# A hybrid recurrent layer on one core: the start in a fixed order on four engines, the first scan's set-up and the output groups moved

## The chip, the cores and the metric

The kernel runs on one core of a Trainium2 chip. A core has five engines that work side by side, each through its own queue of instructions in order: TensorE (PE, matrix products; loading the stationary operand is listed apart as PEld), VectorE (DVE), ScalarE (ACT), GpSimd (POOL) and SyncE (SP), which here issues the transfers between DRAM and the on-chip memory. [...] The metric is the device time of one execution in microseconds (us), lower is better.

## The reference

One layer with two mixers runs over a prompt of 1,024 tokens and over 8 samples of 8 tokens each that continue from given states, 1,088 tokens in all, in float32:

```python
xn = rmsnorm(x, g_norm)
proj = xn @ w_in                                  # 1024 -> 7168: xm, zm, om, f, q, i, z
xc, conv_new = causal_conv(xm, conv_buf, conv_w, conv_b); xc = silu(xc)
q, k = xc_h @ w_q, xc_h @ w_k; v = xm_h @ w_v     # 4 heads
gates = concat(q, k, v) @ w_gate + b_gate         # input and forget gate of each head
hm = mlstm_scan(q, k, v, ig, logsigmoid(fg), ...) # chunked; layernorm, om, skip, zm follow
oh = hgrn2_scan(silu(q), k, i, logf, S0)          # 8 heads; rmsnorm, silu(z) follow
y = rmsnorm(x + concat(hm, oh) @ w_out, g_final)  # and the new states
```

`logf` and the second mixer's `k` use lower bounds from a softmax over `lb_param`.

## The kernel before

**Float32 by three products.** A float32 operand is split into a high part of reduced precision (a cast on ACT) and the rest (a subtraction on DVE or POOL); `mm3` (lines 92 to 96) makes high x high, high x low and low x high, accumulated in PSUM. So every operand costs a cast and a subtraction before PE can use it. `wraw`, `whi` and `wlo` are the raw weights and their two parts, in three, two and two buffers; `XH` and `XL` are the two parts of the turned and normed x.

**The start.** Nine tiles of x (128 tokens each, the last 64) come in by SP in an order fixed by `ordered` (line 188): x 0, the constants, `gB` (g_norm spread over 128 partitions by the transfer itself), x 1, x 2, two weight blocks, x 3 to x 8. `x_norm` (line 220) squares on ACT, takes the root on POOL and scales by `gB` on DVE (L229); `x_split` turns the tile on PE (L241), casts it into `XH` on ACT (L245) and puts the rest into `XL` on DVE (L246). Behind them come the parameter rows (`PR`, turned into `PAR`), the lower bounds (`LB`, `OML`, lines 327 to 335), the convolution's and the norm's history (`hist`) and the gate weights (`wgr`, `wgf`).

**The blocks.** `in_block` (line 270) makes 128 of the 7,168 projected columns for all tokens, in three chunks of 384, 384 and 320 tokens (a block is 72 matmuls of eight k steps), and hands each chunk to an `evac`. It loads the block after next and splits the next. The first eight blocks are `xm`, two for each of four heads. `front_conv` (line 453) makes them: ACT copies a chunk into `xmh` and `XB`, DVE makes `xml` (L470); behind the whole block stand the convolution (one L483 and three L486 on DVE), a sigmoid on ACT (L492), the gating on DVE (L494) and the split into `xch`, `xcl` (L498 on POOL). The first call makes two blocks side by side, the others one.

**The heads.** `qkv_prep` (line 384) loads a head's `w_q`, `w_k`, `w_v`, splits them (`wqh`, `wql`) and appends to the value weights the columns that give the gates: turn `w_v` (L402), copy `wT`, multiply by the gate weights (L406), copy `gv` (L409), turn it (L411), cast into `wqh` (L414) and `wql` (L415). `front_v` makes the values of nine token tiles and the gates' first part, `front_qk` queries and keys, and `gate_part` (a burst of small matmuls) the rest of the gates.

**The scans and the output.** Twelve jobs follow (eight `hgrn_main`, four `mlstm_main`); `weave` lets the blocks of the next job run between a job's own small matmuls. `gate_scan` (line 557), which carries the gates of all four mLSTM heads through DRAM and scans them on DVE, runs inside the first job, whose first level needs `Q1`, `K1` and `Sf` (lines 994 to 1014) from DVE. The output product runs in two halves of 512 columns (`hf`), nine token tiles and two groups of k steps each (`out_part`), whose operands `mix_prep` loads and splits (L1302, L1303); `out_done` adds the last k step and the residual, `wo_prep` loads and splits two k steps of `w_out`. The first five tiles of the first half (`EARLY`) run inside the last job.

**Who sets the order.** The program is written down in one sequence, and a planner with a timeline of its own orders each engine's queue from it. `behind`, `inorder`, `burst` and `issue_after` add constraints of order between two instructions of one engine. Under `tc.manual_schedule(engines=...)` the listed engines keep the written order; before the change that holds for PE alone, from the scans on (line 1441).

## Time and profile before

| | us |
|---|---|
| median of 3 runs | 1157.92 |
| range of these runs | 1155.51 to 1158.99 |
| the profiled execution | 1159.27 |
| its span, first to last instruction | 1157.5 |

The page gives PE 1121.6 us busy (97% of the span), DVE 745.1, ACT 467.9, POOL 259.7. In the views below a row of the order of time reads: start, duration, engine, line, operation, written<-read, count, and in brackets the idle time of the engine before it and what ended that. A row of stretches reads: stretch, its length, busy time and instructions of each engine, the granted clock of TensorE as a share, the share of the DMA engines' time, GB/s. A group's row reads: count, busy us in all, mean ns of one, idle time before.

### The profile page before, as it was taken

The page shows a single profiled execution, that of the slowest core. Times are in us where ns is not written, and L with a number is a line of the kernel's source. Part 1 is how long each engine was busy: PE and PEld are TensorE (multiplying, and loading weights), DVE is VectorE, ACT ScalarE, POOL GpSimd, SP SyncE. Part 2 cuts the span into 40 slices and gives each one's busy share as a digit, 9 for nine tenths or more (in the row PEclk, how much of TensorE's full clock was granted, in tenths as well). Part 3 has the DMA queues.
Part 4 walks back from the last instruction along what each step waited for, and adds up shares of the span by engine and source line. Part 5 has one row for each costly group of instructions (what it writes and reads, how often), then busy time and mean ns, then how long its engine had stood idle before and what let it go on. Part 6 is the DMA issues. An engine that isn't in the chain of part 4 may idle for free.

```text
span 1157.5 us, 22938 instructions
## 1 busy us (share of the span) xinstructions
PE 1121.6 (97%) x9251; PEld 1055.4 (91%) x9251; DVE 745.1 (64%) x1474; ACT 467.9 (40%) x1045; POOL 259.7 (22%) x403
## 2 busy tenths in 40 slices
PE   5889999999999999999999999999999999999997
PEld 5789999899999999999999999999999997878886
DVE  4665354394778667784779567877676686644543
ACT  5454454434532444235423453252524354333332
POOL 4352443102530044203530153102020200100000
PEclk9889999999999999999999999999999999999999
DMA  7234343213324152323224331422222255576662
GB/s 250 56 122 143 119 144 126 71 50 117 103 76 146 54 167 73 122 94 127 64 78 151 116 112 60 133 76 77 56 77 56 76 175 144 156 215 177 188 190 93
DMA packets 154296, 134.05 MB, mean 116 GB/s; under 512 B 11515, under 2 KB 130391, under 8 KB 154190
## 3 DMA queue, kind: packets, MB, share of 16 engines
q1 hardware_dynamic: 154190, 132.59, 36.6%
q8 instruction: 73, 1.20, 0.4%
q14 instruction: 33, 0.27, 0.1%
HBM read 93.99 MB, written 38.57 MB: 115 GB/s over the span
## 4 chain that ended last, share of the span: by engine, by line
PE 84%; DVE 6%; DMA 5%; ACT 3%; issue 2%; POOL 0%; SPq 0%; POOLq 0%; DVEq 0%; ACTq 0%
PE mm L94 23%; PE mm L95 23%; PE mm L96 23%; PE lv L101 2%; DMA mraw<-mixd 2%; DMA woraw<-in_w_out 2%; PE o L1190 1%; PE o L1209 1%; PE o L94 1%; PE o L96 1%; PE o L95 1%; PE o L1212 1%; DVE mlo L1303 1%; PE lv L1171 1%; PE o L1104 1%
## 5 line engine op out<-in xcount | busy, mean ns | idle before, releaser
L94 PE MATMUL mm<-XH,whi 128*128 128x384 f32 (+1 forms) x1344 | 450.1, 335 | 2.2 <-DVE xml L470 2.0
L95 PE MATMUL mm<-XL,whi 128*128 128x384 f32 (+1 forms) x1344 | 440.0, 327 | 0.0
L96 PE MATMUL mm<-XH,wlo 128*128 128x384 f32 (+1 forms) x1344 | 439.5, 327 | 0.0
L94 PEld LDWEIGHTS mm<-XH,whi 128*128 128x128 f32 x1344 | 253.8, 189 | 4.8 <-DVE xml L470 2.2
L95 PEld LDWEIGHTS mm<-XL,whi 128*128 128x128 f32 x1344 | 253.7, 189 | 1.6 <-issue 1.3
L96 PEld LDWEIGHTS mm<-XH,wlo 128*128 128x128 f32 x1344 | 253.2, 188 | 0.0
L147 POOL TENSOR_TENSOR wlo<-wraw,whi 128x1024 fp32r<-128x1024 f32 x34 | 83.1, 2445 | 104.7 <-ACT whi L147 104.6
L147 ACT CAST whi<-wraw 128x1024 fp32r<-128x1024 f32 x56 | 58.8, 1050 | 94.5 <-PE mm L95 74.6
L948 POOL MEMSET A<- 128x288 f32 x8 | 2.7, 343 | 261.4 <-ACT A L1077 261.4
L1302 ACT CAST mhi<-mraw 128x1024 fp32r<-128x1024 f32 (+1 forms) x32 | 31.8, 997 | 66.5 <-PE mm L95 42.8
L96 PE MATMUL mm<-XH,mlo 128*128 128x512 f32 x144 | 56.5, 392 | 2.1 <-DVE mlo L1303 2.1
L94 PE MATMUL mm<-XH,mhi 128*128 128x512 f32 x144 | 56.9, 395 | 1.2 <-ACT mhi L1302 1.2
L95 PE MATMUL mm<-XL,mhi 128*128 128x512 f32 x144 | 56.1, 390 | 0.0
L1303 DVE TENSOR_TENSOR mlo<-mraw,mhi 128x1024 fp32r<-128x1024 f32 (+1 forms) x32 | 37.0, 1156 | 20.6 <-ACT mhi L1302 19.4
L470 DVE TENSOR_TENSOR xml<-mm,xmh 128x384 fp32r<-128x384 f32 (+1 forms) x24 | 12.3, 511 | 50.9 <-ACT XB L469 47.9
L896 DVE TENSOR_SCALAR f<-f,OML,LB 128x384 f32<-128x384 f32 (+1 forms) x24 | 32.8, 1368 | 12.0 <-ACT f L894 11.6
L1371 POOL TENSOR_TENSOR rs<-rs,mhalf 128x1 f32<-128x1 f32 (+1 forms) x9 | 4.9, 542 | 148.5 <-DVE rs L1370 148.5
L96 PE MATMUL mm<-woh,mlo 128*128 128x512 f32 x96 | 37.5, 390 | 0.1
L95 PE MATMUL mm<-wol,mhi 128*128 128x512 f32 x96 | 37.4, 389 | 0.0
L94 PE MATMUL mm<-woh,mhi 128*128 128x512 f32 x96 | 37.3, 389 | 0.0
L486 DVE SCALAR_TENSOR_TENSOR Y<-XB,PAR,Y 128x1112 f32<-128x1112 f32 x24 | 36.8, 1533 | 0.3
L964 DVE TENSOR_TENSOR QK<-hk,Sf 128x256 f32<-128x256 f32 x96 | 36.2, 419 | 0.0
(355 smaller groups left out, 2188.3 us busy)
## 6 DMA issues: line engine op xcount, KB each, us to landing
wraw<-in_w_in SPq DMA_DIRECT2D x56, 512.0 KB
woraw<-in_w_out SPq DMA_DIRECT2D x16, 512.0 KB
mraw<-mixd SPq DMA_DIRECT2D x16, 512.0 KB
mraw<-mixd SPq DMA_DIRECT2D x16, 448.0 KB
xcd<-XB SPq DMA_DIRECT2D x8, 544.0 KB
qkd<-qk SPq DMA_DIRECT2D x16, 272.0 KB
xcr<-xcd SPq DMA_DIRECT2D x8, 544.0 KB
mixd<-xcr SPq DMA_DIRECT2D x8, 544.0 KB
```

The costliest lines, as they stand in the source:

```text
L94: PE.matmul(out, lhsT=lh, rhs=rh, start=first, stop=False)
L95: PE.matmul(out, lhsT=lh, rhs=rl, start=False, stop=False)
L96: PE.matmul(out, lhsT=ll, rhs=rh, start=False, stop=last)
L101: i = PE.matmul(out, lhsT=lhsT, rhs=rhs, start=start, stop=stop)
L147: return S.copy(hi, raw), eng.tensor_tensor(lo, raw, f32(hi), op=ALU.subtract)
L470: evs.append(V.tensor_tensor(ml[:, t0:t0 + m], ps[:, :m], f32(mh[:, t0:t0 + m]), op=ALU.subtract))
L486: V.scalar_tensor_tensor(Y[:, :1112], XB[:, j:j + 1112], cw[:, 8 * j + ft:8 * j + ft + 1], Y[:, :1112], op0=ALU.mult, op1=ALU.add)
L896: V.tensor_scalar(f[:, s], f[:, s], scalar1=OML[:, h:h + 1], scalar2=LB[:, h:h + 1], op0=ALU.mult, op1=ALU.add)
L964: i = V.tensor_tensor(dst, ksrc, ssrc, op=ALU.mult)
L1104: PE.transpose(pt[:, u * P:(u + 1) * P], iT[:, t * P:(t + 1) * P], ident)
L1302: S.copy(hi[:, :w * n], raw[:, :w * n])
L1303: V.tensor_tensor(lo[:, :w * n], raw[:, :w * n], f32(hi[:, :w * n]), op=ALU.subtract)
```

## The change

It has these parts.

- **g_norm:** 4 KB go into one partition on ACT's queue (`g1`); two matmuls with a row of ones spread them over 128 partitions, and DVE copies them into `gB`. x 3 is loaded ahead of the second weight block.
- **The start up to the fourth block's end** is written as one sequence and kept on PE, ACT, DVE and POOL. `x_norm` and `x_split` become `x_square`, `x_scale`, `x_turn` and `x_low`; tiles 3 to 8 stand between the k steps of the first two blocks, and so do the parameter rows, the history, the gate weights and each step of `qkv_prep(0)`. The convolutions are generators (`convolve`), whose steps stand among the matmuls that follow.
- **Work between engines:** the low parts of the first three weight blocks and of block 3, head 0's `xcl`, and head 1's `wql` are made on DVE instead of POOL. `qkv_prep(1)`, the second head's, is spread over the third and fourth block; its casts, its turning and its products stand at four places. For the heads behind it, the second step (the splits) follows the load at once, as before.
- **The lower bounds** are made behind the fourth head's gate columns (`ctxs["cast"]`), beside `masks`; the gate biases are loaded behind the fourth block, the parameter rows behind the last x.
- **The scans' set-up:** the first DVE operation of `gate_scan`'s second step stands behind the copy into `Sf` of the first job (`ctxs["k2"]`).
- **The output:** `out_part` makes the operands of the next group ahead of its own matmuls; tiles 5 to 8 of the first half run one after the other with `out_done` of two earlier tiles and two `wo_prep` behind each; `g_final` is loaded ahead of them.

```diff
+    g1 = unit("g1")
+    nc.scalar.dma_start(out=g1[0:1, :DM], in_=g_norm)
-            lambda: nc.sync.dma_start(out=gB[:, :DM], in_=g_norm.to_broadcast([P, DM])), lambda: x_load(1), lambda: x_load(2),
-            lambda: blk_load(0), lambda: blk_load(1), *[lambda t=t: x_load(t) for t in range(3, 9)])
+    last_x = ordered(lambda: x_load(0), lambda: nc.sync.dma_start(out=CF, in_=c_f32), lambda: x_load(1), lambda: x_load(2),
+            lambda: blk_load(0), lambda: x_load(3), lambda: blk_load(1), *[lambda t=t: x_load(t) for t in range(4, 9)])
...
+        behind(V.tensor_tensor(lbm, lbr[:, 0:8], lbr[:, 8:16], op=ALU.max), ctxs["cast"])
...
-        G.tensor_tensor(wl[:, :512], wr[:, :512], f32(wh[:, :512]), op=ALU.subtract)
-        G.tensor_tensor(wlv[:, :, :256], wrv, f32(whv[:, :, :256]), op=ALU.subtract)
+        eng = V if h == 1 else G
+        eng.tensor_tensor(wl[:, :512], wr[:, :512], f32(wh[:, :512]), op=ALU.subtract)
+        eng.tensor_tensor(wlv[:, :, :256], wrv, f32(whv[:, :, :256]), op=ALU.subtract)
...
-            G.tensor_tensor(cl[:, :T], xc[:, :T], f32(ch[:, :T]), op=ALU.subtract)
+        (V if h == 0 else G).tensor_tensor(cl[:, :T], xc[:, :T], f32(ch[:, :T]), op=ALU.subtract)
...
-        V.tensor_tensor(lm[0:4, :], lfs, m0t, op=ALU.add)
+        behind(V.tensor_tensor(lm[0:4, :], lfs, m0t, op=ALU.add), ctxs["k2"])
...
-        mx = ctxs.pop("mix0") if (hf, t, g) == (0, 0, 0) else mix_prep(t, g)
+        mx = mixes.pop((hf, t, g), None) or mix_prep(t, g)
+        if ahead:
+            mixes[ahead] = mix_prep(*ahead[1:])
...
+    with tc.manual_schedule(engines={ET.PE, ET.Activation, ET.DVE, ET.Pool}):
+        ones = g1[0:1, DM:U]
+        G.memset(ones, 1.0)
+        for i in range(2):
+            pt = ps_o()
+            PE.matmul(pt, lhsT=ones, rhs=g1[0:1, i * 512:(i + 1) * 512], start=True, stop=True)
+            V.tensor_copy(gB[:, i * 512:(i + 1) * 512], pt)
+        x_square(0)
+        x_square(1)
+        x_scale(0)
+        x_square(2)
+        x_turn(0)
+        x_scale(1)
+        x_low(0)
+        low = split_high(0)
+        x_turn(1)
+        x_scale(2)
+        x_low(1)
+        low()
+        x_square(3)
+        x_turn(2)
+        x_low(2)
+        x_square(4)
+        low = split_high(1)
+        x_scale(3)
+        low()
+        convs = []
+        first = front_conv(0, (0, 1), convs)
+        run(islice(first, 1))
+        x_turn(3)
+        x_scale(4)
+        x_low(3)
+        x_square(5)
+        run(islice(first, 2))
...
+        x_turn(8)
+        x_low(8)
+        next(prep)
+        par_turn()
+        hist_turn()
+        gate_weights()
+        run(islice(first, 3))
+        next(prep)
+        run(islice(first, 2))
+        next(prep)
+        run(islice(first, 2))
+        blk_split(2, V)
+        run(prep)
+        c0, c1 = convs
+        next(c0)
+        run(islice(first, 4))
+        run(first)
+        next(c0)
+        next(c1)
+        run(front_v(0))
+        next(c0)
+        convs = []
+        third = front_conv(1, (2,), convs)
+        prep = qkv_prep(1)
+        next(prep)
+        run(islice(third, 2))
+        next(c0)
+        next(c1)
+        run(islice(third, 2))
+        next(c1)
+        run(c0)
+        next(c1)
+        run(islice(third, 4))
+        run(c1)
+        next(prep)
+        run(islice(third, 4))
+        run(third)
+        c2, = convs
+        next(prep)
+        front_qk(0)
+        next(c2)
+        next(prep)
...
+        for t in range(EARLY, 9):
+            part_of(0, t)
+            for n in (t - 1, t - EARLY):
+                out_done(0, n)
+                for i in islice(wos, 1):
+                    wo_prep(1, i)
```

## The prediction

> **What bounds the kernel now.** I read four views in this order: the page (shares, slices, chain), the waits of TensorE alone, the busy time of stretches that I cut at the clock's changes, and the order of time around each stall.

> ```profile
> span 1157.5 us, 22938 instructions
> PE   5889999999999999999999999999999999999997
> PE 84%; DVE 6%; DMA 5%; ACT 3%; issue 2%; POOL 0%; SPq 0%; POOLq 0%; DVEq 0%; ACTq 0%
> ```

> TensorE (PE) carries 84% of the chain that ended last, and only the first three slices and the last are not full. So a microsecond that PE stands still is a microsecond of the span, and one saved on another engine is none. Who makes PE wait (us in all, times, longest):

> ```profile
> PE lv L241 <- DVE xsq L229: 12.4, 4, 9.7
> PE mm L94 <- DVE wqh L414: 3.3, 1, 3.3
> PE lv L101 <- DVE K L961: 2.3, 1, 2.3
> PE mm L96 <- DVE mlo L1303: 2.1, 3, 1.0
> PE mm L94 <- DVE xml L470: 2.0, 1, 2.0
> PE o L411 <- DVE gv L409: 1.4, 1, 1.4
> PE mm L94 <- ACT mhi L1302: 1.2, 1, 1.2
> PE mm L95 <- DVE wql L415: 0.6, 1, 0.6
> ```

> All of it is at the start, at the first scan (L101) and in the output (L1302, L1303): the three places that the change touches. The stretches show what the start loses:

> ```profile
> core 0: us, PE busy (x) PEld busy (x) DVE busy (x) ACT busy (x) POOL busy (x), PEclk, DMA share, GB/s
> 0.00:17.47 17.47, 5.70 (x25) 4.71 (x25) 6.28 (x8) 9.65 (x15) 5.92 (x14) 1.00 0.93 307
> 17.47:39.97 22.50, 20.99 (x135) 19.27 (x134) 16.33 (x21) 14.20 (x29) 10.55 (x18) 1.00 0.46 118
> 39.97:46.80 6.83, 5.06 (x16) 5.06 (x17) 3.76 (x14) 1.99 (x6) 2.30 (x16) 0.50 0.27 77
> 46.80:60.45 13.65, 9.98 (x64) 8.94 (x62) 7.12 (x7) 4.43 (x10) 7.09 (x5) 1.00 0.14 41
> 60.45:67.28 6.83, 5.24 (x22) 4.99 (x23) 4.59 (x10) 4.01 (x8) 1.60 (x2) 0.50 0.26 77
> 67.28:71.72 4.44, 4.21 (x35) 4.00 (x34) 4.41 (x2) 3.07 (x15) 3.36 (x1) 1.00 0.80 304
> 71.72:106.00 34.28, 34.28 (x231) 32.38 (x230) 14.43 (x21) 15.62 (x34) 11.68 (x22) 1.00 0.33 112
> ```

> At 17.47 the first block's matmuls begin, at 71.72 those of the third; between lie two blocks, the transposes of x tiles 3 to 8, the first head's gate weights and its value projection. Idle time there is 1.51 + 1.77 + 3.67 + 1.59 + 0.23 = 8.8 us. Two stretches run at a granted clock of 0.50: half of 5.06 + 5.24 us busy, 5.2 us, is lost to it. From 71.72 on PE is full, so nothing is to be had there.

> **The first matmul.** These rows set it:

> ```profile
> 8.36 1.28 DVE L229 SCALAR_TENSOR_TENSOR xsq<-x,ss,gB 128x1024 f32<-128x1024 f32 x1 [8.36 <-DMA gB<-in_g_norm]
> 9.69 1.06 ACT L227 ACTIVATE xsq<-x 128x1024 f32<-128x1024 f32 x1 [4.33 <-DMA x<-in_x_prompt]
> 9.71 1.11 PE L241 MATMUL lv<-CF,xsq 128*128 128x128 f32 x4 [9.71 <-DVE xsq L229]
> 18.27 0.61 PE L95 MATMUL mm<-XL,whi 128*128 128x384 f32 x1
> 24.17 0.60 PE L241 MATMUL o<-CF,xsq 128*128 128x128 f32 x4
> L406 PE MATMUL o<-wT,front 128*8 128x256 f32 x8 | 2.1, 380 | 0.0
> L229 DVE SCALAR_TENSOR_TENSOR xsq<-x,ss,gB 128x1024 f32<-128x1024 f32 x8 | 10.3, 1284 | 14.7 <-DMA gB<-in_g_norm 8.4 <-POOL ss L200 6.3
> L246 DVE TENSOR_TENSOR XL<-lv,XH 128x512 fp32r<-128x512 f32 x8 | 5.5, 687 | 2.5 <-ACT XH L245 2.5
> ```

> DVE waits until 8.36 for g_norm, 512 KB in a stage where the DMA engines are full (0.93, 307 GB/s), and ACT until 9.69 for the second x tile behind it. The change loads 4 KB and spreads it on PE: two products of 512 columns. L406 gives 2.1 / 8 = 0.26 us for 256 columns and one of two passes, so 0.5 us for 512; four of them at the start's half clock (four transposes take 1.11 at 9.71, 0.60 at 24.17) are 4.2 us at most. No row shows the 4 KB landing; the first x tile, 512 KB, was squared by 5.36 (9.69 - 4.33), so it had landed by 4.3, and I put the 4 KB at 2 to 4. With the copies (0.69 each by L246) gB is ready between 6 and 9; I take 7.5. The 512 KB gone bring the second tile 1.7 us forward, to about 8. From 7.5 DVE must do three scalings, six low halves and the first weights' low half before the second matmul: 3 x 1.28 + 6 x 0.69 + 1.23 = 9.2, with half a microsecond of waits 17.2. That is the 18.27 row: **1.1 us earlier** (bounds -0.5 and 2.5).

> **From there to the third block.** Before: 71.72 - 17.47 = 54.25 us, minus 8.8 idle, minus 5.2 at half clock and some 1.0 more at its beginning (the 18.27 row is still slow), leaves 39.3 us of work at full clock. What stalls PE in the middle:

> ```profile
> 56.55 3.17 POOL L147 TENSOR_TENSOR wlo<-wraw,whi 128x1024 fp32r<-128x1024 f32 x1 [0.33 <-ACT whi L147]
> 57.77 3.12 DVE L486 SCALAR_TENSOR_TENSOR Y<-XB,PAR,Y 128x1112 f32<-128x1112 f32 x1
> 61.15 0.16 DVE L414 CAST wqh<-o 128x16 fp32r<-128x16 f32 x1
> ```

> The gate columns' 0.16 us cast stands on DVE behind a convolution step that takes 3.12 us where the same operation on 1,024 columns takes 1.28 (L229): it runs against a POOL split of 3.17. In the new order the whole chain (wT, gv, casts) lies between steps of the second block's matmuls, ahead of the first convolution, and the third block's split goes to DVE (1.23 us as a row below has it). The parameter tables, too, are turned between matmuls, not in one stretch, after which PE stood the 2.0 us of the L470 row. So 8.8 + 5.2 are free to go. What comes instead: the clock must open after 17.2, one or two stretches of 3.4 us (half of the 6.83 that each half-clock stretch lasted), 1.7 to 3.4 lost, I take 2.1; DVE is just short of the fourth x tile and of the value projection's third tile, 1.4 (0 to 3). Then the third block starts at 17.2 + 39.3 + 2.1 + 1.4 = 60.0, not 71.72: **11.7 us earlier**.

> [...]

> [...]

> **To the fourth block's end** the order is fixed too, and PE was full before; here it can only lose. Ahead of the first query product DVE has, from the end of the value projection: five operations on two operands of some 1,000 columns (a split, two gatings, two low halves that POOL had; 1.23 each by the split at 229.12 below), two convolution steps (1.28 each as L229), and six of 512 columns or fewer (at most 0.69 as L246): 12.9 us. The third block's 72 matmuls take 10.7 at the 34.28 / 231 = 0.148 of the last stretch. **1.6 us lost** (0 to 3). And the gate product now stands directly behind the last query matmul and waits for ACT's evacuation of it, 272 columns, which I bound by the 0.43 of L903 for 320 and two hand-overs: **0.6 lost**. Before, another block's matmuls stood between. Start together: 11.7 - 2.2 = 9.5 us.

> **The first scan.**

> ```profile
> 226.44 0.43 ACT L903 ACTIVATE hq<-mm 128x320 f32<-128x320 f32 x1
> 226.82 0.15 DVE L576 TENSOR_TENSOR lm<-glf,m0t 4x8 f32<-4x8 f32 x1 [2.18 <-DMA glf<-gd]
> 229.12 1.23 DVE L147 TENSOR_TENSOR wlo<-wraw,whi 128x1024 fp32r<-128x1024 f32 x1 [0.32 <-issue]
> 230.26 0.48 DVE L904 TENSOR_TENSOR hq<-hq,mm 128x320 f32<-128x320 f32 x1
> 231.41 0.49 DVE L961 COPY K<-hk 128x256 f32<-128x256 f32 x2
> 232.05 0.65 PE L101 MATMUL lv<-Q,K 128*32 128x64 f32 x32 [2.27 <-DVE K L961]
> ```

> From 224.64 (226.82 - 2.18) to 229.12 DVE stands, but for small operations, for the gates' way through DRAM, with the first level's operands queued behind; PE waits 2.27 from 229.78 on. The change puts the gate operations behind the level's last copy (the Sf copy). The DMA has landed by then, so the wait is not moved but covered: from 226.87, where ACT is done with the last q chunk, the split, L904, the product between them (231.41 - 230.74) and the copies need 1.2 + 0.5 + 0.7 + 0.5 = 2.9 us and end by 229.8. **2.2 us saved** (0 to 2.4). The gate scan itself is wanted only by the mLSTM head after this one.

> **The output.**

> ```profile
> 1010.00:1034.00 24.00, 24.00 (x107) 19.88 (x106) 9.10 (x12) 8.22 (x16) 0.00 (x0) 1.00 0.83 260
> 1035.84 0.50 PE L94 MATMUL mm<-XH,mhi 128*128 128x512 f32 x1 [1.22 <-ACT mhi L1302]
> 1037.29 0.50 PE L96 MATMUL mm<-XH,mlo 128*128 128x512 f32 x1 [0.71 <-DVE mlo L1303]
> ```

> A group's operands are split when PE wants them: 1.2 + 0.7 us. One group ahead is 5.4 us of matmuls (24 at 24.00 / 107 = 0.224), which covers a split; the weights' loads still share three raw buffers and a DMA stage at 0.83. **1.5 saved** (-1 to 2.5). The other 1.4 us of the L1303 row lie in the early groups, which keep their old form.

> **Small terms.** The lower bounds move behind the fourth head's casts, so an Exp falls between Sigmoids, two table loads more:

> ```profile
> L492 ACT ACT_TABLE_LOAD x1 | 1.3, 1283 | 1.1 <-DVE wql L415 1.1
> ```

> They are hidden by ACT's slack (15.62 busy of 34.28 in a comparable stretch); uncovered, 2.6. I take **0.5 lost**. The gate biases' five small loads and the conv and parameter loads go later on SP; each is wanted behind the first two blocks' matmuls, and what it came later than those would be lost one for one. g_norm's load stands on ACT's queue ahead of the table load, in time that ACT has.

> **The sum.** 9.5 + 2.2 + 1.5 - 0.5 = 12.7 us. The profiled execution took 1159.27 (span 1157.5 and 1.8 around it), 1.35 above the median of the runs, 1157.92. So 1146.6 for an execution like it, and **1145** against the median. The bounds at one end, 14 + 2.4 + 2.5, give 1139; at the other 3 + 0 - 1 - 2.6, no change.

> **Rivals.** (1) *The new order has waits of its own.* Nothing slips past a late transfer or a late DVE result on four queues now; each missed 3.4 us stretch at half clock costs 1.7. Three such and a second qk wait halve the start: gain 4 to 8, 1150 to 1154. For it: DVE paces the first 17 us in my own walk; against: 8.8 us of idle time go. Chance 0.20. (2) *The start is given back*: the planner that orders ACT, DVE and POOL after the fourth block finds another order, or a weight load comes late, up to the scans; only the 2.2 and 1.5 stay, less small losses, 1155 to 1160. Against it: from 71.72 PE is full and its suppliers are half idle. 0.06. (3) *Slower, by the clock.* If PE's steps between DVE's results are too short to open the clock, half speed goes on; a stretch with 5.24 of 6.83 busy ran at 0.50. Half clock costs half of the time it lasts, so the 12.7 us are gone after 25 us more of it: if it opens later than about 47. Shut until the third block, it costs 39.3 instead of 2.1: 1182. Against it: the stretch from 39.97 ended at full clock with 1.77 idle in it. 0.06. (4) *All hidden* and the clock early: above 17 gained, below 1141. 0.06. That the change doesn't do what it says would show as (2).

> **Chances.** The forecast's own case, 1141 to 1149, 0.62. The range that leaves about 2 in 10 out is 1138 to 1153. A change within 0.3% (3.5 us) can't be told from none here; faster is the forecast, (1) and (4), 0.88; the same (2), 0.06; slower (3), 0.06.

> **What would show it.** Right: L229's first wait ends before 8; PE's wait for L414 and L415 gone; no stretch of clock 0.50 after 25 us; the first third-block matmul near 60; no wait of PE for L961; the first Q,K burst some 12 us earlier; at 1030, no waits for L1302. Wrong: PE waits of over 1 us between 20 and 60, a clock at 0.50 past 30, or a start 10 us earlier that has shrunk at the first scan.

## The result, and the profile after

| | before | after |
|---|---|---|
| median of 5 runs each | 1158.99 us | 1148.71 us |
| range of these runs | 1155.51 to 1160.74 | 1147.95 to 1151.3 |
| span of the profiled execution | 1157.5 | 1147.7 |

The ratio is 0.9912 with a 95% interval of 0.9899 to 0.9926: 10.3 us faster, where 1145 (1138 to 1153) was forecast. The span shrank by 9.8 us, where the sum had 12.7. First the page of the kernel after (span, TensorE in 40 slices, chain), then those waits of TensorE that bear on the forecast.

```profile
span 1147.7 us, 22956 instructions
PE   7989999899999999999999999999999999999997
PE 88%; DVE 5%; ACT 3%; DMA 2%; issue 2%; POOL 0%; SPq 0%; POOLq 0%; DVEq 0%; ACTq 0%
```

```profile
PE lv L239 <- DVE xsq L222: 4.1, 3, 2.3
PE lv L101 <- DVE K L987: 2.9, 1, 2.9
PE mm L95 <- DVE xcl L522: 2.2, 1, 2.2
PE mm L94 <- ACT GTOK L541: 1.6, 1, 1.6
PE mm L94 <- ACT xch L520: 0.6, 1, 0.6
PE mm L96 <- DVE mlo L1329: 0.2, 1, 0.2
```

The wait for the scaled x tiles shrank from 12.4 to 4.1 us. The waits for the gate columns (3.3, 0.6, 1.4 before) and for the output's high parts (1.2) are gone. K at the first scan is still there, longer, and three waits are new or longer: for head 0's values (GTOK, 0.2 before) and for its first query product (xch, xcl). Stretches of the kernel after, cut at its stages and at the clock's changes, columns as before:

```profile
16.47:20.71 4.24, 3.85 (x15) 3.46 (x15) 3.81 (x5) 2.68 (x5) 2.91 (x5) 1.00 1.11 276
20.71:50.77 30.06, 30.00 (x198) 28.04 (x198) 18.32 (x32) 16.09 (x35) 6.81 (x17) 1.00 0.29 67
50.77:59.38 8.61, 6.99 (x54) 6.76 (x55) 7.65 (x9) 4.35 (x20) 1.97 (x14) 1.00 0.46 153
71.92:75.33 3.41, 0.68 (x4) 0.25 (x2) 1.77 (x3) 3.19 (x7) 0.16 (x1) 1.00 0.41 163
75.33:78.74 3.41, 3.19 (x12) 2.90 (x13) 2.41 (x5) 1.08 (x4) 0.31 (x4) 0.50 0.24 70
222.10:225.51 3.41, 0.48 (x19) 0.28 (x21) 3.21 (x9) 1.53 (x5) 0.00 (x0) 1.00 0.16 42
225.51:228.93 3.42, 3.42 (x85) 3.38 (x75) 3.42 (x6) 0.31 (x2) 0.12 (x1) 0.50 0.37 112
```

The record of the clock begins where it opens, at 20.71, so the row ahead of it reads 1.00 too. That it was still at half there is read from the products of 384 columns: they start 0.32 us apart up to 18.3 and 0.17 apart from 20.77 on. Between 20.71 and 50.77 TensorE is full (30.00 of 30.06 us): the first two blocks with everything that was laid between their steps run without a stop. Then come 1.6 us of idle time in the value projection, and two places where a wait is followed by one stretch of 3.41 us at a granted clock of 0.50. (At the very end, from 1143.70 on, it is 0.50 too, as in the kernel before from 1152.72 on.)

Where the time went, as starts of the same instructions in the order of time of both profiled executions:

| start of | before | after | gain so far | forecast |
|---|---|---|---|---|
| first product with `XL` (L95) | 18.27 | 16.86 | 1.4 | 1.1 |
| third block | 71.72 | 59.38 | 12.3 | 11.7 |
| end of the fourth block | 104.57 | 97.11 | 7.5 | 9.5 |
| last block ahead of the scans | 225.43 | 217.98 | 7.5 | 9.0 |
| first scan job's first Q,K product | 232.05 | 225.26 | 6.8 | 11.2 |
| second scan job | 361.97 | 356.62 | 5.4 | 11.2 |
| last scan job | 927.67 | 921.93 | 5.7 | 11.2 |
| end | 1157.49 | 1147.71 | 9.8 | 12.7 |

The first row is the one that the prediction calls the second matmul; in the kernel before it is the third. Two steps failed: from the third to the fourth block 4.9 us are lost again instead of 2.2, and the first scan loses 2.1 (6.6 to 7.3 us from the last block to the first product, and 1.4 behind it) where it was to win 2.2. The output won 4.0 instead of 1.5, which hides much of both. Each of these places follows, the kernel after in order of time where nothing else is said.

**The first scan.**

```profile
222.25 0.07 DVE L604 MEMSET gt<- 4x8 f32 x1 [5.05 <-DMA gt<-gd]
222.33 1.22 DVE L147 TENSOR_TENSOR wlo<-wraw,whi 128x1024 fp32r<-128x1024 f32 x1
225.26 0.90 PE L101 MATMUL lv<-Q,K 128*32 128x64 f32 x32 [2.93 <-DVE K L987]
225.38 0.15 DVE L603 TENSOR_TENSOR lm<-glf,m0t 4x8 f32<-4x8 f32 x1
```

The constraint did what it says: `lm` (L603) stands behind the copies, at 225.38. But the line behind it, a memset of 4x8 into `gt`, depends on nothing that `lm` writes, so nothing moved it. It waits for the same way through DRAM, 5.05 us, with the split, the last q chunk, Q and K queued behind it. The kernel before had shown this wait, behind that of `lm`:

```profile
227.95 0.07 DVE L577 MEMSET gt<- 4x8 f32 x1 [0.77 <-DMA gt<-gd]
```

That the step lost time, and did not merely fail to win any, lies in that way itself. SyncE issues the first read only when the last write has landed (in the profiles it waits 1.5 us for that landing before, 3.3 after), and that took longer in the kernel after. The first two rows are of the kernel before (1.87 us from issue to issue), the last two of the kernel after (3.73):

```profile
222.75 0.32 SPq L568 DMA_DIRECT2D gd<-lg  x1
224.62 0.27 SPq L570 DMA_DIRECT2D glf<-gd  x1
215.30 0.32 SPq L595 DMA_DIRECT2D gd<-lg  x1
219.03 0.27 SPq L597 DMA_DIRECT2D glf<-gd  x1
```

Why the write took longer is not known. In the run of experiment 5, with the same order at the scan, it took 1.77 us, TensorE waited 1.0 us for K, and the step lasted 5.34 us instead of 7.28.

**The query product.**

```profile
60.04 1.28 ACT L514 ACT_TABLE_LOAD   x1
62.44 1.03 ACT L147 CAST whi<-wraw 128x1024 fp32r<-128x1024 f32 x1
63.51 1.23 DVE L147 TENSOR_TENSOR wlo<-wraw,whi 128x1024 fp32r<-128x1024 f32 x1 [4.54 <-ACT whi L147]
73.56 0.56 DVE L479 TENSOR_TENSOR xml<-mm,xmh 128x384 fp32r<-128x384 f32 x1 [1.92 <-ACT XB L478]
74.03 1.28 DVE L522 TENSOR_TENSOR xcl<-XB,xch 128x1088 fp32r<-128x1088 f32 x1
75.37 0.60 PE L95 MATMUL mm<-xcl,wqh 128*128 128x272 f32 x1 [2.15 <-DVE xcl L522]
```

VectorE stands 4.54 us for the cast of block 3's weights, which stands on ScalarE behind a table load and the sigmoid, does that split, and only then head 0's gating; at 73.56 it stands again, 1.92 us, with the second `xcl` queued behind.

**The values.**

```profile
51.64 1.38 DVE L506 SCALAR_TENSOR_TENSOR Y<-XB,PAR,Y 128x1112 f32<-128x1112 f32 x1
52.94 0.41 DVE L479 TENSOR_TENSOR xml<-mm,xmh 128x256 fp32r<-128x256 f32 x1
53.38 0.22 ACT L481 COPY XB<-mm 128x64 f32<-128x64 f32 x1 [1.99 <-DVE xml L479]
54.16 0.39 PE L94 MATMUL mm<-wqh,xmh 128*128 128x264 f32 x1 [1.61 <-ACT GTOK L541]
```

The first values' copies (L540, L541) stand on ScalarE behind a copy that waits for an `xml`, and that stands on VectorE behind two convolution operations.

### The profile page after: what moved, and what is told of

Its sections match the earlier page's. It is cut to its first block, busy times and chain, and to the rows that moved or that the text cites. A ratio compares the mean times of both kernels' runs of the same rounds, so it can differ in the third digit from the quotient of the medians.

```text
span 1147.7 us, 22956 instructions
## 1 busy us (share of the span) xinstructions
PE 1123.9 (98%) x9255; PEld 1056.0 (92%) x9255; DVE 749.7 (65%) x1484; ACT 471.1 (41%) x1047; POOL 239.7 (21%) x396
## 4 chain that ended last, share of the span: by engine, by line
PE 88%; DVE 5%; ACT 3%; DMA 2%; issue 2%; POOL 0%; SPq 0%; POOLq 0%; DVEq 0%; ACTq 0%
PE mm L94 24%; PE mm L95 23%; PE mm L96 23%; PE lv L101 2%; PE o L1216 1%; PE o L1235 1%; PE o L94 1%; PE o L95 1%; PE o L96 1%; PE o L1238 1%; DMA mraw<-mixd 1%; PE lv L1197 1%; PE o L1130 1%; PE mm L1338 1%; PE mm L1340 1%
## 5 line engine op out<-in xcount | busy, mean ns | idle before, releaser
L94 PE MATMUL mm<-XH,whi 128*128 128x384 f32 (+1 forms) x1344 | 450.4, 335 | 0.0
L95 PE MATMUL mm<-XL,whi 128*128 128x384 f32 (+1 forms) x1344 | 439.4, 327 | 0.4 <-DVE XL L245 0.4
L96 PE MATMUL mm<-XH,wlo 128*128 128x384 f32 (+1 forms) x1344 | 439.2, 327 | 0.0
L94 PEld LDWEIGHTS mm<-XH,whi 128*128 128x128 f32 x1344 | 253.5, 189 | 3.1 <-issue 2.5
L95 PEld LDWEIGHTS mm<-XL,whi 128*128 128x128 f32 x1344 | 253.5, 189 | 1.8 <-issue 0.9
L96 PEld LDWEIGHTS mm<-XH,wlo 128*128 128x128 f32 x1344 | 252.9, 188 | 0.0
L147 ACT CAST whi<-wraw 128x1024 fp32r<-128x1024 f32 x54 | 56.7, 1051 | 87.2 <-PE mm L95 67.2
L147 POOL TENSOR_TENSOR wlo<-wraw,whi 128x1024 fp32r<-128x1024 f32 x30 | 71.8, 2392 | 84.3 <-ACT whi L147 84.0
L1328 ACT CAST mhi<-mraw 128x1024 fp32r<-128x1024 f32 (+1 forms) x32 | 31.9, 998 | 69.3 <-PE mm L95 50.5
L94 PE MATMUL mm<-XH,mhi 128*128 128x512 f32 x144 | 56.8, 395 | 0.0
L96 PE MATMUL mm<-XH,mlo 128*128 128x512 f32 x144 | 56.3, 391 | 0.2 <-DVE mlo L1329 0.2
L95 PE MATMUL mm<-XL,mhi 128*128 128x512 f32 x144 | 56.1, 389 | 0.0
L1329 DVE TENSOR_TENSOR mlo<-mraw,mhi 128x1024 fp32r<-128x1024 f32 (+1 forms) x32 | 37.0, 1155 | 20.2 <-ACT mhi L1328 19.7
L922 DVE TENSOR_SCALAR f<-f,OML,LB 128x384 f32<-128x384 f32 (+1 forms) x24 | 32.9, 1369 | 10.7 <-ACT f L920 10.3
L479 DVE TENSOR_TENSOR xml<-mm,xmh 128x384 fp32r<-128x384 f32 (+1 forms) x24 | 12.3, 511 | 42.2 <-ACT XB L478 42.2
L96 PE MATMUL mm<-woh,mlo 128*128 128x512 f32 x96 | 37.5, 390 | 0.0
L147 DVE TENSOR_TENSOR wlo<-wraw,whi 128x1024 fp32r<-128x1024 f32 x24 | 29.3, 1220 | 12.5 <-ACT whi L147 12.5
L94 PE MATMUL mm<-woh,mhi 128*128 128x512 f32 x96 | 37.4, 389 | 0.0
L95 PE MATMUL mm<-wol,mhi 128*128 128x512 f32 x96 | 37.4, 389 | 0.0
```

Of the source, the lines that this page charges most:

```text
L94: PE.matmul(out, lhsT=lh, rhs=rh, start=first, stop=False)
L95: PE.matmul(out, lhsT=lh, rhs=rl, start=False, stop=False)
L96: PE.matmul(out, lhsT=ll, rhs=rh, start=False, stop=last)
L147: return S.copy(hi, raw), eng.tensor_tensor(lo, raw, f32(hi), op=ALU.subtract)
L479: evs.append(V.tensor_tensor(ml[:, t0:t0 + m], ps[:, :m], f32(mh[:, t0:t0 + m]), op=ALU.subtract))
L922: V.tensor_scalar(f[:, s], f[:, s], scalar1=OML[:, h:h + 1], scalar2=LB[:, h:h + 1], op0=ALU.mult, op1=ALU.add)
```

## The experiments

All are edits of the kernel after; ratios are against the kernel before on the same chip (the kernel after: 0.9912). The interval of a ratio is 1.5 to 3 us wide on each side, and a stretch at half clock falls in one execution and not in the next; so the size of a part is read as the distance between two instructions of one profile, with the ratio beside it. Such a distance varies too: over the profiles whose order is that of the kernel after in the part in question, the query product lasts 11.08 to 13.19 us (six profiles; the kernel after is the short end, with one stretch at half clock where the others have two), and the last scan job's start to the end 224.86 to 227.16 (ten). A single difference of 1 to 2 us at these two places proves little by itself.

**1. The memset behind the copy too.**

```diff
-        V.memset(t1[:, TP:T].rearrange("p (b c) -> p b c", c=8)[:, :, 0], -1e30)
+        behind(V.memset(t1[:, TP:T].rearrange("p (b c) -> p b c", c=8)[:, :, 0], -1e30), ctxs["k2"])
```

> The changed kernel with one more constraint: the small memset of gt (4x8, L604) also stands behind the copy into Sf. Theory: at the first scan the wait of the gates' way through DRAM was never covered, because this memset of 0.07 us stayed ahead of the split, hq, Q and K on VectorE, and it waits for the same transfer (5.05 us idle before it at 222.25). With it behind the copy, VectorE splits at once, TensorE's wait of 2.93 us for K at L101 is gone, and so is the stretch of 3.41 us at a granted clock of 0.50 that follows it (225.5 to 228.9, half of it lost, 1.7 us): the second scan job starts at 352.0 instead of 356.62, the span is 1143.1 instead of 1147.7. Rival: something else holds the level's operands (the cast of the raw weights, the last q chunk on ScalarE) and takes the wait over; then L101 still waits over 1 us, for K or Q, and the span stays between 1146 and 1148.

Ratio 0.9883 (0.9862 to 0.9903), 1145.47 us, span 1144.8. VectorE and TensorE at the first scan:

```profile
219.59 1.22 DVE L147 TENSOR_TENSOR wlo<-wraw,whi 128x1024 fp32r<-128x1024 f32 x1 [1.93 <-ACT whi L147]
222.73 0.49 PE L101 MATMUL lv<-Q,K 128*32 128x64 f32 x20
222.75 0.07 DVE L604 MEMSET gt<- 4x8 f32 x1
```

TensorE no longer waits. The last block to the first product is 4.28 us instead of 7.28, and the first job 129.96 instead of 131.36 (no stretch at half clock): 4.4 us, the theory. It is no chance of one execution: with this edit the distance is 4.28 in all five profiles that have it, with the constraint as first written 5.34 to 7.28 in seven. The span is 1.7 longer than expected; of that, 1.5 is the query product, which had two half-clock stretches instead of one (74.25 to 81.07). Which operations a constraint names decided the step, not the idea behind it.

**2. The constraint taken away.**

```diff
-        behind(V.tensor_tensor(lm[0:4, :], lfs, m0t, op=ALU.add), ctxs["k2"])
+        V.tensor_tensor(lm[0:4, :], lfs, m0t, op=ALU.add)
```

> The changed kernel without the constraint of gate_scan's first operation behind the copy into Sf. Theory: the constraint alone moved nothing that TensorE feels, since the memset next to it kept the wait; without it VectorE waits for the transfers ahead of the same split, and three more small operations (0.15 us each) stand ahead of Q and K. TensorE waits 2.9 to 3.5 us for K, and the distance from the last block before the scans to the first level's first product is 7.2 to 7.8 us (7.28 in the changed kernel, 6.62 before). Rival: the constraint covered a part, and without it the wait is over 4 us; or it did harm, and the distance is 6.6 again.

One execution, span 1148.4. The wait is 3.29 us and the distance 7.65, as the theory has it. Against the kernel after that is 0.4 us for the constraint as written; but the write to DRAM was quicker here (3.34 us to the first read instead of 3.73), and with this taken off each distance the constraint is worth 0.8. Its stretches around the wait, which the section on the hardware takes up:

```profile
222.07:225.48 3.41, 1.85 (x11) 1.53 (x9) 1.70 (x6) 0.00 (x0) 0.00 (x0) 1.00 0.03 7
225.48:228.90 3.42, 1.69 (x84) 1.69 (x85) 3.39 (x7) 1.86 (x6) 0.00 (x0) 1.00 0.53 152
228.90:232.31 3.41, 3.41 (x22) 3.41 (x21) 3.41 (x10) 0.00 (x0) 2.13 (x6) 1.00 0.02 6
```

**3. The query product: block 3's split out of the chain.**

```diff
         next(prep)
+        low = split_high(3)
         run(islice(third, 2))
...
-        run(islice(third, 4))
         run(c1)
+        run(islice(third, 4))
...
         next(prep)
+        low()
         front_qk(0)
```

> The changed kernel with the order of two things altered ahead of the first query product: the low part of block 3's weights, 1.23 us on VectorE, stands behind the second head's weight work instead of ahead of head 0's first gating, and the second xcl stands ahead of the third block's second xml. Theory: the fourth block ends 4.9 us later than the third block's gain would give because VectorE's chain to the second xcl is late by the 2.15 and 0.61 us that TensorE waits at 72 to 75, and because these waits bring one stretch of 3.41 us at half clock (1.7 us). With the split out of the chain all of it moves 2 us forward: the waits shrink to under 0.7 together, no stretch at 0.50 is left between 60 and 100, the fourth block ends near 93 instead of 97.11, and the span is 1143.5 (1142.5 to 1145.5). Rival: the chain is set by ScalarE's sigmoid and its table load (60.04 to 62.54), with the split only standing in idle time; then the second xcl ends less than 0.8 us earlier, the stretch at half clock stays and the span is 1147 to 1148.

Ratio 0.9879 (0.9858 to 0.99), 1145.04 us, span 1143.6. The query product lasts 7.66 us instead of 11.08, no stretch at half clock is left there, and the fourth block ends at 93.62. The edit does two things: it moves the split, and it puts the second `xcl` ahead of the third block's second `xml`. Of the 3.56 us by which that `xcl` starts earlier (70.47 against 74.03), 2.35 are there at head 0's first gating already (62.30 against 64.65), so they are the split's; the other 1.2 come with the new place. One wait stays:

```profile
PE mm L94 <- DVE xml L483: 1.3, 1, 1.3
```

The theory holds, with a rest that experiment 8 takes up.

**4. The values: the first convolution behind the last xml.**

```diff
-        next(c0)
         run(islice(first, 4))
         run(first)
         next(c0)
+        next(c0)
```

> The changed kernel with head 0's first two convolution operations behind the second block's last xml instead of ahead of it. Theory: TensorE's wait of 1.61 us in the value projection (52.55) comes from ScalarE, whose copies of the first values stand behind a copy that waits for that xml on VectorE, behind 2.2 us of convolution. With the order changed the wait is gone and the third block starts at 57.8 instead of 59.38. What follows later is the question: the chain to the second xcl starts no earlier on VectorE, which has the same operations to do, but its idle time there was 4.5 us before the third block's split. If the sigmoids move forward with the value copies, the query product's stall stays as it is and the span is 1146.1; rival: the chain does not move, TensorE comes to the query product 1.6 us earlier and waits there 1.6 us longer, and the span stays at 1147.5 to 1148.

Ratio 0.9916 (0.9891 to 0.9942), 1150.01 us, span 1147.7. The value projection lasts 7.02 us instead of 8.49, so the wait's cause is right. But the query product lasts 12.00 instead of 11.08, and the fourth block ends at 97.00 (97.11), as the rival has it (counted from the second block's end, which came later here, 46.18 against 46.71). The rival's mechanism is not what the profile shows, though: the chain moved with TensorE (table load at 59.00 instead of 60.04), and the waits for xch and xcl are the same 0.62 and 2.16. What grew is a third wait, for the PSUM buffer (`mm`, of which the kernel has three) that the third block's last xml reads, from 0.18 to 1.10: TensorE came to it some 1.3 us behind the start of the `xcl` product (an estimate from the rows of VectorE and the 1.10), where the same eight products took 2.18 in the kernel after, in its stretch at 0.50; and it is 1.11 in the run without the group ahead (experiment 7) too, whose start is that of the kernel after. So the 0.9 most likely belongs to the place of the clock's stretch; it is within the 11.08 to 13.19 above, and this run alone doesn't settle what the edit is worth; experiment 8 does.

**5. g_norm spread by its transfer again.**

```diff
-    nc.scalar.dma_start(out=g1[0:1, :DM], in_=g_norm)
+            lambda: nc.sync.dma_start(out=gB[:, :DM], in_=g_norm.to_broadcast([P, DM])), lambda: x_load(1), lambda: x_load(2),
...
-            PE.matmul(pt, lhsT=ones, rhs=g1[0:1, i * 512:(i + 1) * 512], start=True, stop=True)
-            V.tensor_copy(gB[:, i * 512:(i + 1) * 512], pt)
```

> The changed kernel with g_norm spread over the 128 partitions by its transfer again (512 KB), in the old place of the queue, and without the two products and copies. Theory: the 4 KB transfer is what brought the second product of the first block from 18.27 to 16.86; with the 512 KB back VectorE's first scaling waits until 8.4, the second product is near 18.3 and the third block starts 1 to 1.5 us later, near 60.6. Rival: the first product is set by the x tiles and the first weights, which come in the same stage; then the second product stays within 0.5 us of 16.86.

One execution, span 1149.4: the first product with `XL` at 18.78, the third block at 61.29, 1.9 us later each, somewhat more than expected.

```profile
8.69 1.28 DVE L221 SCALAR_TENSOR_TENSOR xsq<-x,ss,gB 128x1024 f32<-128x1024 f32 x1 [8.69 <-DMA gB<-in_g_norm]
```

In the kernel after the same operation starts at 6.94. The theory holds; the 4 KB way is the cause.

**6. The third block's low part on POOL again.**

```diff
-        blk_split(2, V)
+        blk_split(2, G)
```

> The changed kernel with the low part of the third block's weights on POOL again instead of VectorE. Theory: VectorE is free 1.2 us earlier, but runs its first convolution beside POOL's split, and there a scalar_tensor_tensor of 1112 columns took 3.12 us in the kernel before, 1.38 in the changed one; so the two convolution operations ahead of the second block's last xml take over 4 us instead of 2.2, TensorE's wait in the value projection is 2 to 3.5 us instead of 1.61 and the third block starts at 60 to 61.5 (a stretch at half clock included). Rival: the operations of the two engines do not disturb each other here, VectorE comes to that xml 1.2 us earlier, and the third block starts at 58.2.

One execution, span 1151.1. VectorE and POOL:

```profile
48.77 2.60 POOL L147 TENSOR_TENSOR wlo<-wraw,whi 128x1024 fp32r<-128x1024 f32 x1 [7.45 <-ACT whi L147]
49.15 3.40 DVE L506 SCALAR_TENSOR_TENSOR Y<-XB,PAR,Y 128x1112 f32<-128x1112 f32 x1
51.31 1.27 POOL L500 COPY front<-XB 128x3 f32<-128x3 f32 x1
```

The step takes 3.40 us beside the split, where it takes 1.38 by itself (51.64 in the kernel after), and ends 1.18 after it; POOL's next copy, of three columns, then takes 1.27, until VectorE is through (the like copy at 52.81 takes 0.18). TensorE waits 2.14 us in the values instead of 1.61, the clock falls (mean of the execution 0.992, in the kernel after 0.995), and the third block starts at 60.43, 10.64 us behind the second's end instead of 8.98. So the move to VectorE is worth 1.7 us here, the clock's stretch included. The rows show that both operations are long where they overlap; what makes them so they do not show.

**7. The output: the old loop, and the new sequence without the group ahead.** The first edit puts the old loop back, the second keeps the new one but for the line that makes the next group's operands.

```diff
-        for t in range(EARLY, 9):
-            part_of(0, t)
-            for n in (t - 1, t - EARLY):
-                out_done(0, n)
...
+        for t in range(9):
+            out_done(0, t)
+            if 3 <= t < 7:
+                run(chain(out_part(0, t + 2, 0), out_part(0, t + 2, 1)))
```

```diff
-                run(out_part(hf, t, g, nexts[hf, t, g]))
+                run(out_part(hf, t, g))
```

> The changed kernel with the output loop of the kernel before: no group made ahead, the old sequence of the out_done and wo_prep calls, g_final loaded at the old place. Start and scans are those of the changed kernel. Theory: the output part is worth the 4.0 us by which the distance from the last scan job's start to the end shrank (229.82 to 225.78), of which 1.21, 0.71 and 0.14 us are waits of TensorE for operands of L1302 and L1303 from 1034 on and 0.98 plus 0.41 were waits in the early groups at 962 to 969; the span is 1151.7. Rival: the early groups' 1.2 us came from the shift of the start against the transfers, not from the output loop; then only 2.1 to 2.8 come back and the span is 1149.8 to 1150.5.

> The changed kernel with its new sequence of output parts, out_done and wo_prep, but each group's operands made when the group comes, as before. The old output loop cost 2.11 us from the last scan job's start to the end (227.89 against 225.78). Theory: it is the group ahead that covers the splits, so TensorE's waits for L1328 and L1329 near 1030 (1.2 and 0.7 us) are back and the distance is 227.5 to 228. Rival: the sequence does it (a long run of parts ahead of the out_done calls gives ScalarE and VectorE the time); then the distance stays at 225.8 to 226.2 and the group ahead is worth nothing.

The old loop: ratio 0.9947 (0.9923 to 0.997), 1153.49 us. Without the group ahead: 0.9942 (0.9921 to 0.9963), 1152.71 us. From the last scan job's start to the end, before 229.82, after 225.78, with the old loop 227.89, without the group ahead 227.50. The ratios, 4.0 and 3.5 us above that of the kernel after, leave both theories open; both profiles had two stretches at half clock at the query product. By the distance the loop is worth 2.1 us, not 4.0: the rival. The other 1.9 came without it; the old loop's profile has the waits near 1030 back and none of the 0.98 and 0.41 at 962 to 969. At like early tiles the loop is worth more: in the runs of edits 3 and 4 TensorE waits for no operand there either, and the distance is 224.87 and 224.86, 3.0 us shorter than with the old loop. The old loop's waits:

```profile
PE mm L94 <- ACT mhi L1328: 1.2, 1, 1.2
PE mm L96 <- DVE mlo L1329: 0.9, 2, 0.7
```

Without the group ahead, neither theory is right as it stood. 1.72 us are lost, but the waits near 1030 are not what is lost:

```profile
PE lv L1197 <- DVE S L1270: 1.7, 2, 1.1
PE mm L96 <- DVE mlo L1329: 0.6, 2, 0.4
```

Of the first row 0.6 lies near 288, as in the kernel after; the 1.1 are at 1002, within the last job. Why that state came later there was not settled, and so not how much of the 1.72 is the group ahead's own. What the profile does show is that the splits near 1030 are covered without the group ahead, so by the new sequence; the one wait for a low part that is left in the output is 0.21 at 1019.

**8. Three orders, four, and the gate columns later.** Edits 1, 3 and 4 together; then also the second head's splits behind the first query product; then also its last step (L420 and two casts) one chunk later. The second and the third edit:

```diff
         run(c1)
-        run(islice(third, 4))
-        next(prep)
-        run(islice(third, 4))
+        run(islice(third, 8))
         run(third)
         c2, = convs
-        next(prep)
         low()
         front_qk(0)
+        next(prep)
+        next(prep)
         next(c2)
-        next(prep)
```

```diff
-        run(prep)
         next(c2)
         run(islice(fourth, 2))
         run(c2)
-        run(islice(fourth, 4))
+        run(islice(fourth, 2))
+        run(prep)
         run(fourth)
```

> The changed kernel with the three orders of the runs before together: the memset behind the copy into Sf, the second xcl's chain without block 3's split, and head 0's first convolution behind the second block's last xml. Theory: the first two add up (4.4 at the first scan, 3.5 at the query product) and the third, which brought nothing alone because TensorE only came earlier to a chain that was late, now brings its 1.5 us less what the query product still waits for; the fourth block ends near 92.3 (93.62 with the second alone), the span is 1138.5. Rival: the third is worth nothing here either, since the 1.34 us wait that the query product keeps grows by what is won; the fourth block ends at 93.5, the span is 1139.5 to 1140.5.

> As the run with three orders, and the second head's splits (two casts, two low parts) and the turning of its value weights stand behind the first query product instead of ahead of it. Theory: the 1.34 us wait that is left in the query product is for a PSUM bank, held by the third block's last xml, which stands behind these low parts (1.37 us) on VectorE; with them gone it falls under 0.3 us, and the fourth block ends near 91 and the span is 1137.2. Rival: the splits only change place, and the fourth block or the second head's gate columns wait for them (TensorE waits of over 0.5 us for L414, L417 or wqh between 80 and 97); the span is then that of the three orders or longer.

> As the run with four orders, and the last step of the second head's gate columns (turning gv, L420, and its two small casts) one chunk of the fourth block later. Theory: with four orders TensorE waits 1.95 us at 86.25 for gv, which VectorE copies behind three convolution operations and an xml, and loses a stretch of 3.41 us at half clock behind it; with six products of 320 columns ahead of L420 and gv copied by then no wait stays, and the fourth block ends 3.5 us earlier, at 92.0 to 92.3 against 95.52 (the query product lasts 6.73 us, as with four orders). The span is 1137 to 1139. Rival: the second head's value projection then waits for the late gate columns by more than 0.5 us, and the span stays over 1139.5.

| | ratio | median, us | query product | second to fourth block's end |
|---|---|---|---|---|
| after | 0.9912 | 1148.71 | 11.08 | 46.71 |
| edit 3 alone | 0.9879 | 1145.04 | 7.66 | 43.33 |
| three orders | 0.9838 (0.9818 to 0.9859) | 1140.4 | 7.65 | 41.88 |
| four orders | 0.9859 (0.9835 to 0.9883) | 1143.83 | 6.73 | 44.77 |
| gate columns later | 0.9838 (0.9824 to 0.9851) | 1140.77 | 6.73 | 41.2 |

With three, edit 4 brings its 1.45 us (43.33 to 41.88), having brought 0.5 alone: the theory, in its place. (The value projection is 7.02 us in all five profiles with edit 4 and 8.47 to 8.49 in the seven others with the third block's split on VectorE.) The span, 1140.6, missed 1138.5 by 2.1; 1.4 of that lie behind the last scan job's start (experiment 9). With four the last query wait goes and a new one comes, 1.95 us for `gv`, which VectorE copies behind four convolution operations and an `xml` at 87.74; the clock falls on it:

```profile
86.43:89.84 3.41, 1.64 (x10) 1.62 (x11) 3.00 (x6) 1.20 (x2) 0.00 (x0) 1.00 0.00 0
89.84:93.25 3.41, 3.41 (x14) 3.41 (x13) 0.89 (x3) 1.96 (x3) 1.87 (x1) 0.50 0.41 163
```

That is the rival: the span is 1142.1, not 1137.2. Order is not the whole of it. The first of the four convolution operations ran beside a split on POOL and took 2.64 us, where it takes 0.85 by itself (50.76 in the kernel after), and VectorE has no idle time from there to `gv`. So the overlap, as in experiment 6, makes 1.8 (2.64 less 0.85) of the 1.95 us:

```profile
80.12 2.39 POOL L147 TENSOR_TENSOR wlo<-wraw,whi 128x1024 fp32r<-128x1024 f32 x1
80.48 2.64 DVE L503 TENSOR_SCALAR Y<-XB,PAR 128x1112 f32<-128x1112 f32 x1
```

With the last step later the wait is gone and 3.57 us are back (44.77 to 41.2); the span is 1138.1, within what was expected. The fourth block ends at 90.52, earlier than expected, since the second block ended 1.4 us earlier than with four orders (49.32 against 50.75) in this execution, whose clock opened at 15.66.

**9. The residual requested early.** In the output's early tiles the residual's transfer goes ahead of the tile's products.

```diff
         for t in range(EARLY):
+            if t < STORED:
+                out_load(t)
             for g in range(2):
```

> As the run before it in this list, and the residual rows of the first four early output tiles are requested ahead of the tile's products instead of behind them. Theory: the waits of TensorE for mlo in the early groups (0.98 and 0.41 us in the kernel before, 0.85 and 0.42 with three orders, 0.22 in the changed kernel) come from VectorE, where the addition of the residual waits for its transfer with the next group's low part queued behind; so they depend on when the transfer lands and not on the output loop. With the transfer requested earlier VectorE's waits for it are under 0.2 us and TensorE waits under 0.5 us in all between the last scan job's start plus 30 and plus 50, and the run is 0.5 to 1.2 us faster than without. Rival: the low parts are late for ScalarE or for their own transfers, and the waits stay.

Ratio 0.9825 (0.9809 to 0.984), 1139.96 us, span 1137.8. With three orders VectorE had stood like this:

```profile
946.31 0.69 DVE L1371 TENSOR_TENSOR xr<-xr,mm 128x512 f32<-128x512 f32 x1 [2.38 <-DMA xr<-in_x_prompt]
948.19 1.08 DVE L1329 TENSOR_TENSOR mlo<-mraw,mhi 128x896 fp32r<-128x896 f32 x1
```

Now it waits for neither transfer in that stretch, and TensorE for no `mlo`. The last job's start to the end is 224.89 us, against 226.04 with the gate columns later, which lacks this edit alone, and 227.16 with three orders. That is the theory, and the profiles without the edit bear it out: with the loop of the kernel after, TensorE waits for an early `mlo` wherever VectorE stands 0.97 us or more for that transfer, and nowhere where it stands 0.70 or less. So the edit makes sure of what some executions had by the transfer's early landing (224.86 and 224.87 in the runs of edits 4 and 3). By the medians the gain (0.8 us) can't be told from none. This run, the one with late gate columns and the one with three orders are the fastest here, by their ratios some 8.5 to 10 us ahead of the kernel after. In two stretches of this run's profile, from the clock's opening on, TensorE hardly stands any more:

```profile
20.67:91.66 70.99, 70.66 (x469) 65.69 (x467) 47.65 (x65) 38.98 (x91) 12.85 (x46) 1.00 0.38 116
216.00:912.00 696.00, 694.38 (x6575) 676.79 (x6574) 506.37 (x1124) 272.73 (x640) 168.02 (x253) 1.00 0.30 94
```

## Why the prediction was right, and where it was not

The time fell within the range and 3.7 us above the point (1.1 of it because the kernel before measured 1158.99 over five runs, not 1157.92), but the sum is right in part by luck, by terms that cancelled: misses of 4.3 (first scan) and 2.7 (fourth block) against 2.5 (output), 0.6 (third block), 0.5 (table loads) and 0.4 between the scan jobs make the 2.9 us by which 9.8 falls short of 12.7.

- **First matmul, 1.1 earlier: right (1.4).** In the kernel after the 4 KB had landed at 2.25 (forecast 2 to 4), the four products (the trace has two for each of the two calls) took 3.75 (at most 4.2), gB was ready at 6.73 (7.5). VectorE then stood 1.98 us for the second tile's root, where 0.5 of waits were put; one low half fewer stood ahead of the product. Experiment 5 shows the cause.
- **Third block at 60.0: right (59.38), term by term but one.** The clock opened at 20.71, which cost 1.9 (forecast 2.1; the 3.4 us of a stretch, there half of 6.83, are 3.41 here, 75.33 to 78.74), and the rest is 39.0 us of work (39.3). The stall of 1.4 was put on VectorE's x tile and third value; what came is 1.61 at the third value, where ScalarE's copies wait for VectorE, and no wait at the fourth x tile. POOL's two halves of head 0's low weights, which ran beside VectorE's parameter copies, held up nothing: those copies took 0.24, 0.34 and 0.18 us beside a half of 1.29 (from 38.28 on).
- **To the fourth block's end, 2.2 lost: wrong (4.9).** The term that failed is VectorE's 12.9 us against 10.7 (a difference of 2.2, not the 1.6 written). Both sizes were off: the block's 72 matmuls took 11.8 us (59.38 to 71.22), and from there to the second `xcl`'s end, 59.38 to 75.31, VectorE is busy 9.9. Back to back, as the prediction took them, these operations would have cost TensorE nothing. What it left out is that they wait for ScalarE (4.54 + 1.92 idle), which the chain runs through twice. TensorE's waits there are 0.61 + 2.15 + 0.18 = 2.9, and the clock's stretch at 0.50 adds 1.7; the price of a stretch stood in the prediction (1.7, half of 3.41) but only for the clock's opening and in the rivals. Experiment 3 shows both. The 4.9 is the short end: five other profiles with this order have two stretches there and a query product 1.4 to 2.1 us longer. The 0.6 for the gate burst has no row after.
- **First scan, 2.2 saved: wrong (2.1 lost).** The step that failed is "the gate operations behind the level's last copy": one of them was put there, not the memset next to it, whose transfer lands later than `glf`'s. Experiments 1 and 2 show this; with the memset moved the step wins 2.3 at the first product (6.62 to 4.28), about what was forecast. That it lost 0.7 there instead is the slower write to DRAM (3.73 us against 1.87), the other 1.4 the stretch at half clock behind the wait.
- **Output, 1.5 saved: mis-sized.** The loop is worth 2.1, or 3.0 at like early tiles. That "one group ahead" covers the split isn't what was seen: without it the splits near 1030 are covered too (experiment 7). "The other 1.4 us lie in the early groups, which keep their old form" was true of the form and wrong of the time: 1.2 of these waits went away unedited, because they hang on when a transfer lands (experiments 7 and 9).
- **Table loads, 0.5 lost: nothing.** The trace has the two more (17 of 1.28 us, against 15), but from the fourth block's end to the last block ahead of the scans it is 120.86 before and 120.87 after.
- **Clock.** "No stretch of clock 0.50 after 25 us" was wrong twice. Rival (1), waits of the new order's own, is what came, at two places instead of three; the output's unforeseen gain kept the time in the forecast's case, 0.3 us inside its edge.

## What to carry to other kernels

When a constraint is to take work off a path, list every instruction of that step that waits for the same event, however small, and look for the ones that depend on none of the others. A chain over two engines in fixed order is costed by walking both queues together, since the sum of one engine's operations leaves out each hand-over. Where single executions differ by where the clock falls, size an edit by a distance within the profile, see how far that distance varies between profiles in which the part is the same, and try the edits of one stretch together before one that shows little is dropped.

## What the runs showed of the hardware

In the stretch of 3.41 us ahead of a fall to 0.50 TensorE had been idle for 0.56 and 3.12 us in the kernel before (ahead of 39.97 and 60.45), for 2.73 and 2.93 in the kernel after (rows above: 0.68 and 0.48 busy of 3.41), and for 1.77 with four orders (1.64 busy). Behind stretches of that length with 1.34 (before, 227.71 to 231.12), 1.61 (after, 51.43 to 54.85), 1.56 and 1.73 us of idle time (experiment 2, 1.85 and 1.69 busy) it stayed at 1.00. In experiment 2 a wait of 3.29 us, longer than the 2.93 of the kernel after, fell across two stretches; it cost itself alone, as did the 2.27 of the kernel before (1.00 from 227.71 to 234.53), while the 2.93 cost 1.7 more, an estimate: half of the 3.41 at 0.50 behind it. The 0.56 us ahead of 39.97 stand among small transposes (36.18 to 39.75). What else tells these stretches apart the runs do not show, and what counts as busy was not tried.
